# A LayerNorm's mean as two matmuls, placed later in a gemm stream, and one low weight part made by VectorE instead of by a DMA

## The chip, the core and the metric

The kernel runs on one core of a Trainium2 chip. The metric is the device time of one execution in microseconds (us); lower is better. The engines carry the names of the profile: PE is TensorE (PEld its weight loads), DVE is VectorE, ACT is ScalarE, POOL is GpSimd, SP is SyncE, which here only issues DMAs.

## The reference, cut to what matters

One layer of a decoder trunk on 288 tokens (256 of a new sequence and 8 times 4 of running ones), all in float32.

```python
h = rmsnorm(x, norm1_g)
proj = h @ w_in + b_in                         # 2048 -> 3072
a, gate, z = proj[:, :1024], proj[:, 1024:2048], proj[:, 2048:]
u = a * sigmoid(gate)
c = silu(layernorm(depthwise_causal_conv(u_ext, conv_w, conv_b), ln_g, ln_b))   # 31 taps, 1024 channels
d = multiscale_pool(z_ext)                     # windows 2, 4, 8, 16
p = einsum(d, pool_w) * pool_scale             # 4 groups of 256
x = x + concat([c, p]) @ w_out                 # 2048 -> 2048
x = x + square(relu(rmsnorm(x, norm2_g) @ w_ff1)) @ w_ff2     # 2048 -> 8192 -> 2048
y = rmsnorm(x, norm_f)

def layernorm(x, g, b):
    mu = mean(x); var = mean((x - mu) ** 2)
    return (x - mu) * rsqrt(var + EPS) * g + b
```

The change is in the mean `mu` of this LayerNorm, over the 1024 channels of the convolution, and in how one piece of `w_in` is prepared.

## The kernel before, in words

Channels lie on the 128 partitions and the 288 tokens on the free axis, so every matmul has a 128x128 block of a weight matrix as its stationary side and 288 columns as its moving side. To come near float32, each weight and each activation is split in two parts of type float32r, a high one and a low one, and a product is three matmuls: high by high, low weight by high, high weight by low.

**Weights.** A weight block of 1024 rows and 256 columns comes in two halves (`load`, 512 KB each, issued by SP into the six buffers `wr`). `split_part` makes `whi` and `wlo` of a half; there are five buffers of each. ACT always makes `whi` with a cast (L260). The table `WAYS` says who makes `wlo`, half by half: `G` is POOL (two subtractions of 128x512, L268), `V` is DVE (one subtraction of 128x1024, L265), and `D` is ACT and a DMA: ACT writes the negative of `whi` into `wlo` (L262), and POOL issues a DMA that adds the weights from memory to it (L263). `turns` counts the halves of a stage, so `"c3": "GDGD"` stands for the four halves of the fourth conv projection, c3.

**Stages.** `SEQUENCE` sets the order of the input projections: c0 to c7 are pairs of a conv and a gate tile (`conv_products`, then `conv_pair`), p3 to p0 the pooling groups, P3 to P0 their small products. A `gemm` runs over k in pairs of two; one such step of two banks is 12 matmuls. In the conv tail (priority `later`) DVE applies the 31 taps of tile i one after another (L426, the tiles `pc` and, for the last tap, `c`). POOL adds finished pairs of conv tiles into `sum_c` (L435), up to tile 5.

**The output projection and the LayerNorm.** The output product is cut in two. First come eight gemms (g = 0 to 7) with the pooling half `mixp` (`dx` in the rows); each writes one pair of PSUM banks `ac` and is added to `xT` by DVE (L549). Into this stream the LayerNorm is woven: `BETWEEN` names, by gemm and k, where PE runs the matmul of the mean (`ln_mean`), the matmuls of the sum of squares (`ln_sums`, then a chain of small steps on DVE and ACT for the reciprocal root) and the matmuls that spread the result over the partitions (`ln_rows`). After the eight gemms the normalised tiles `mixc` (`mx` in the rows) are made by DVE and ACT (L554 to L560), and eight more gemms with `mixc` follow. Then the MLP, four chunks of 2048, and the final norm.

**What sets the order.** The program is put into each engine's queue by a list scheduler that follows its own estimate of times and the priorities; each engine then works through its queue in that order. So a small edit moves instructions far from it. The PSUM pool `acc` has two pairs of banks: a gemm can start when the xT add of the gemm two before it is done.

Of the kernel before, what the change touches and what calls it, by code (L numbers as in the profile page):

```python
# [12 lines left out]
ALU = mybir.AluOpType  # L13
# [17 lines left out]
N8 = DC // P  # L31
# [35 lines left out]

WAYS = {"c2": "GVGV", "c3": "GDGD", "c4": "GDGD", "p3": "GDDG", "c5": "GDGD", "c": "GGGV", "p": "GVVG", "w": "GG", "ff": "VV"}  # L70


VEC = (("norm1_g", 16), ("b_in", 24), ("conv_b", 8), ("ln_g", 8), ("ln_b", 8), ("pool_scale", 8), ("norm2_g", 16), ("norm_f", 16))
# [10 lines left out]
def trunk_kernel(ctx: ExitStack, tc: tile.TileContext, io):  # L84
# [3 lines left out]
    nc = tc.nc  # L88
# [14 lines left out]
    def nm(s):  # L103
        seen[s] = seen.get(s, 0) + 1
        return f"{s}{seen[s]}"

    @contextmanager
    def later(by=LATER):

        tc.cur_priority += by  # L110
        yield
        tc.cur_priority -= by
# [15 lines left out]
    def ms(name):  # L128
        return msp.tile([P, 2, 512], F32, name=nm(name), tag="ms")
# [8 lines left out]
    def samples(ap, n):  # L138
        return ap.rearrange("p (b t) -> p b t", t=n)
# [8 lines left out]
    def v(key, j):  # L148
        return vec[:, OFF[key] + j : OFF[key] + j + 1]
# [45 lines left out]
    ones = const.tile([P, P], F32, name="ones")  # L195
# [3 lines left out]
    def load_table(func, src):  # L199

        nc.scalar.activation(few[: src.shape[0], :], src, func)
# [52 lines left out]
    def split_part(raw, src, hi, lo, way):  # L254

        nc.scalar.copy(hi, raw)  # L260
        if way == "D":
            nc.scalar.activation(lo, f32(hi), AF.Copy, scale=-1.0)  # L262
            nc.gpsimd.dma_start(lo, src, accum_op=ALU.add)  # L263
        elif way == "V":
            nc.vector.tensor_tensor(lo, raw, f32(hi), op=ALU.subtract)  # L265
        else:
            for j in range(0, raw.shape[1], 2):
                nc.gpsimd.tensor_tensor(lo[:, j : j + 2, :], raw[:, j : j + 2, :], f32(hi[:, j : j + 2, :]), op=ALU.subtract)  # L268

    def spl():  # L270
        return [wspl.tile([P, 4, 256], F32R, name=nm("w" + part), tag="w" + part) for part in ("hi", "lo")]
# [4 lines left out]
    def split(halves, stage="ff"):  # L276

        parts = []
        for raw, src in halves:
            turns[stage] = turns.get(stage, -1) + 1  # L280
            parts.append(spl())
            ways = WAYS.get(stage) or WAYS[stage[0]]
            split_part(raw, src, *parts[-1], ways[turns[stage] % len(ways)])
        return lambda k, m: columns(*parts[k // 4], k % 4, m)

    def gemm(banks, rhs, m_outer=False, between={}, classes=""):


        n = len(rhs)
        gets = ready.pop()  # L290
        step = 2 if len(banks) == 2 else 1
        pairs = [(k, m) for k in range(0, n, step) for m in range(len(banks))]
        if m_outer:
            pairs.sort(key=lambda km: km[1])
        if step == 2:
            parts = ((0, 0, 0), (1, 0, 0), (0, 1, 0), (1, 1, 0), (1, 0, 1), (0, 0, 1))
        else:
            parts = ((0, 0, 0), (0, 0, 1), (0, 1, 0))
        todo = [(k + d, m, w, x) for k, m in pairs for d, w, x in parts]
        head = todo[: len(classes)]  # L300
        for j, c in enumerate(classes):
            todo[j] = next(p for p in head if (p[0] + p[3]) % 2 == int(c))
            head.remove(todo[j])
        ends = {m: [f(j for j, p in enumerate(todo) if p[1] == m) for f in (min, max)] for m in range(len(banks))}
        ahead = None
        for j, (k, m, w, x) in enumerate(todo):
            if j % (len(banks) * len(parts)) == 0:
                ahead = between[k]() if k in between else None
            with tc.issue_after(ahead.ins) if ahead is not None else nullcontext():
                last = nc.tensor.matmul(banks[m][:, :T], gets[k // 8](k % 8, m)[w], rhs[k][x], start=j == ends[m][0], stop=j == ends[m][1])  # L310
        ready.extend(itertools.islice(weights, 1))
        return last.ins
# [4 lines left out]
    def each(bk):  # L317
        return [bk[:, m, :] for m in range(2)]
# [72 lines left out]
    cs, pcs = [], []  # L391
    sum_c = tmpp.tile([P, 2, T], F32, name="sum_c", tag="ag2", bufs=2)
# [10 lines left out]
    def conv_pair(i, banks):  # L403
        up = u_all[:, i, 0:UO]
        us = samples(u_all[:, i, UO:UL], US)
        ta, gate = [b[:, :T] for b in banks]
        for b in (gate, ta):
            nc.vector.tensor_tensor(b, b, rb, op=ALU.mult)
        tg = tmpp.tile([P, 2, T], F32, name=nm("tg"), tag="ag", bufs=2)[:, 0, :]
        nc.scalar.activation(tg, gate, AF.Sigmoid, bias=v("b_in", 8 + i))  # L410
        if i == N8 - 1:
            load_table(AF.Sqrt, tg[:, 0:1])
        for out, a, b in ((up[:, CH:UO], ta[:, :SEQ], tg[:, :SEQ]), (us[:, :, CH:US], samples(ta[:, SEQ:T], NS), samples(tg[:, SEQ:T], NS))):
            nc.vector.scalar_tensor_tensor(out=out, in0=a, scalar=v("b_in", i), in1=b, op0=ALU.add, op1=ALU.mult)
        if i % 2 == 0:
            cs.append(actp.tile([P, 2, T], F32, name=nm("c"), tag="c", bufs=4))
        c = cs[i // 2][:, i % 2, :]
        with later():
            if i % 2 == 0:
                pcs.append(cvp.tile([P, 2, SEQ], F32, name=nm("pc"), tag="cv"))  # L420
            pc = pcs[i // 2][:, i % 2, :]
            cwv = vec[:, CWO + i * CW : CWO + (i + 1) * CW]
            nc.scalar.activation(pc, up[:, 0:SEQ], AF.Identity, bias=v("conv_b", i), scale=cwv[:, 0:1])  # L423
            for w in range(1, CW):
                dst = pc if w < CW - 1 else c[:, 0:SEQ]
                nc.vector.scalar_tensor_tensor(out=dst, in0=up[:, w : w + SEQ], scalar=cwv[:, w : w + 1], in1=pc, op0=ALU.mult, op1=ALU.add)  # L426
            prd = prdp.tile([P, NB, NS, CW + 1], F32, name=nm("prd"), tag="prd")
            nc.scalar.activation(prd[:, :, :, CW], ones[:, 0 : NB * NS].rearrange("p (b t) -> p b t", t=NS), AF.Identity, bias=v("conv_b", i), scale=0.0)
            for t in range(NS):
                nc.gpsimd.tensor_tensor(prd[:, :, t, 0:CW], us[:, :, t : t + CW], cwv[:, None, :].to_broadcast([P, NB, CW]), op=ALU.mult)  # L430
            cso = c[:, SEQ:T]
            nc.vector.tensor_reduce(samples(cso, NS), prd, axis=AX.X, op=ALU.add)
            if i % 2 and 1 < i < N8 - 1:
                for m in range(2):
                    nc.gpsimd.tensor_tensor(sum_c[:, m, :], (cs[0] if i == 3 else sum_c)[:, m, :], cs[i // 2][:, m, :], op=ALU.add)  # L435


    dd = {}
# [58 lines left out]
    with tc.issue_after(gemm(pair0 + pair1, hx, between={15: first_sums})):  # L497
        third = conv_products(2, between={2: first_rows})
    nc.gpsimd.memset(z_all[:, :, 0:PH], 0.0)
    conv_pair(0, pair0)  # L500
    conv_pair(1, pair1)
    conv_pair(2, third)
    for kind, i in SEQUENCE[3:]:
        if kind == "c":
# [10 lines left out]
    norm = {}  # L515

    def ln_mean():
        nc.vector.tensor_tensor(sum_c, sum_c, cs[-1], op=ALU.add)  # L518
        nc.vector.tensor_tensor(sum_c[:, 0, :], sum_c[:, 0, :], sum_c[:, 1, :], op=ALU.add)  # L519
        norm["mean"] = ms("pmean")[:, 0, :T]  # L520
        return nc.tensor.matmul(norm["mean"], ones, sum_c[:, 0, :], start=True, stop=True)  # L521

    def ln_sums():
        ssc = None
# [13 lines left out]
        norm["rows"], last = spread(norm["sums"])  # L538
        return last

    BETWEEN = {4: {4: ln_mean}, 5: {6: ln_sums}, 6: {4: ln_rows}}
    behind = nullcontext()
    for g in range(8):
        bk = bank2()
        with behind:
            last = gemm(each(bk), [mixp[k] for k in korder], between=BETWEEN.get(g, {}))
        behind = tc.issue_after(last) if g > 3 else nullcontext()
# [4 lines left out]
    for j, c in enumerate(cs):  # L552
        n = tmpp.tile([P, 2, T], F32, name=nm("n"), tag="ag", bufs=2)
        nc.vector.tensor_tensor(n, c, norm["rows"][:, None, :].to_broadcast([P, 2, T]), op=ALU.mult)  # L554
        for m in range(2):
            i = 2 * j + m
# [145 lines left out]
```

## Time and profile before

| | |
|---|---|
| median of 3 runs | 1096.75 us (1096.19 to 1097.46) |
| the profiled execution | 1097.78 us, of which the span of the profile is 1096.0 us |
| granted TensorE clock, mean | 0.994 |
| busy: PE, DVE, ACT, POOL | 1077.8, 640.9, 477.5, 179.2 us |
| read from HBM | 185.68 MB, 173 GB/s over the span |

The profile shows one execution. Times in its rows count from the start of the span. A row of the timeline gives start, duration, engine, line, operation, the written tile and the tiles read, and in brackets the idle time of the engine ahead of it with what ended it. A row of the chain of waits gives start, duration and what the end of the program waited on there. A row of windows gives, for a stretch, the busy time and number of starts of each engine, then the granted TensorE clock, the DMA share and GB/s.

### The profile page before, as it was taken

How to read it: one execution, taken by the hardware profiler on the slowest of the kernel's cores; microseconds unless marked ns; L12 is line 12 of the kernel's file. 1: busy time of each engine (PE TensorE's matmuls, PEld its weight loads, DVE VectorE, ACT ScalarE, POOL GpSimd, SP SyncE). 2: the span in 40 equal slices, each digit the busy share in tenths (PEclk: the TensorE clock that was granted, in tenths of full speed). 3: DMA queues.
4: the chain of work that ended last, by engine and by line, in shares of the span. 5: the costliest groups of instructions: out<-in, count | busy, mean ns of one | idle time of the engine just before them, and what ended most of it. 6: DMA issues, size and time to landing. Idle time of an engine off the chain costs nothing.

```text
span 1096.0 us, 19604 instructions
## 1 busy us (share of the span) xinstructions
PE 1077.8 (98%) x8204; PEld 1075.6 (98%) x8204; DVE 640.9 (58%) x814; ACT 477.5 (44%) x585; POOL 179.2 (16%) x209
## 2 busy tenths in 40 slices
PE   8999999899999999999999999999999999999996
PEld 8999999899999999999999999999999999999996
DVE  7889999778554544445554444445544445554553
ACT  8654445365444433334443333444433334444441
POOL 0878989602100000000000000000000000000000
PEclk9999999899999999999999999999999999999998
DMA  9996468455455555555555555555555555555522
GB/s 335 277 271 175 147 166 244 150 159 170 157 169 168 165 171 173 168 169 166 171 171 168 167 168 174 168 167 168 171 173 164 169 169 172 171 165 167 171 77 87
DMA packets 58264, 191.23 MB, mean 174 GB/s; under 512 B 6208, under 2 KB 11328, under 8 KB 58176
## 3 DMA queue, kind: packets, MB, share of 16 engines
q1 hardware_dynamic: 56752, 185.53, 54.0%
q0 software_dynamic: 1152, 4.19, 2.1%
q8 instruction: 64, 1.05, 0.4%
q10 hardware_dynamic: 272, 0.26, 0.1%
q14 instruction: 24, 0.20, 0.0%
HBM read 185.68 MB, written 4.28 MB: 173 GB/s over the span
## 4 chain that ended last, share of the span: by engine, by line
PE 95%; DMA 1%; DVE 1%; POOL 1%; issue 1%; ACT 0%; SPq 0%; DVEq 0%; POOLq 0%
PE ac L310 93%; DMA wlo<-in_w 1%; POOL wlo L268 1%; PE pp L310 0%; DVE xT L642 0%; DMA wr<-in_w 0%; POOL prd L430 0%; DVE sum_c L518 0%; PE pt L225 0%; ACT whi L260 0%; PE idle L228 0%; PE pt L245 0%; DVE sum_c L519 0%; PE pmean L521 0%; DVE wlo L265 0%
## 5 line engine op out<-in xcount | busy, mean ns | idle before, releaser
L260 ACT CAST whi<-wr 128x1024 fp32r<-128x1024 f32 (+1 forms) x341 | 355.1, 1041 | 566.2 <-PE ac L310 544.9
L265 DVE TENSOR_TENSOR wlo<-wr,whi 128x1024 fp32r<-128x1024 f32 (+1 forms) x295 | 363.3, 1232 | 352.5 <-ACT whi L260 352.1
L310 PE MATMUL ac<-ax,whi 128*128 128x288 f32 x2048 | 351.5, 292 | 0.0
L310 PE MATMUL ac<-fx,whi 128*128 128x288 f32 x2048 | 350.4, 292 | 0.0
L310 PEld LDWEIGHTS ac<-ax,whi 128*128 128x128 f32 x2048 | 296.0, 187 | 0.0
L310 PEld LDWEIGHTS ac<-fx,whi 128*128 128x128 f32 x2048 | 295.5, 187 | 0.0
L310 PE MATMUL ac<-ax,wlo 128*128 128x288 f32 x1024 | 217.1, 292 | 0.0
L310 PE MATMUL ac<-fx,wlo 128*128 128x288 f32 x1024 | 216.6, 292 | 0.0
L310 PEld LDWEIGHTS ac<-ax,wlo 128*128 128x128 f32 x1024 | 162.5, 187 | 0.0
L310 PEld LDWEIGHTS ac<-fx,wlo 128*128 128x128 f32 x1024 | 162.1, 187 | 0.0
L310 PE MATMUL ac<-hx,whi 128*128 128x288 f32 x768 | 136.5, 296 | 2.2 <-ACT hx L332 1.5
L310 PEld LDWEIGHTS ac<-hx,whi 128*128 128x128 f32 x768 | 114.0, 189 | 2.8 <-ACT hx L332 1.7
L268 POOL TENSOR_TENSOR wlo<-wr,whi 128x512 fp32r<-128x512 f32 x76 | 104.3, 1420 | 42.4 <-ACT whi L260 41.4
L426 DVE SCALAR_TENSOR_TENSOR pc<-u_all,vec,pc 128x256 f32<-128x256 f32 x232 | 99.7, 483 | 3.2 <-ACT pc L423 1.9
L310 PE MATMUL ac<-hx,wlo 128*128 128x288 f32 x384 | 85.5, 296 | 1.2 <-DMA wlo<-in_w 1.0
L310 PEld LDWEIGHTS ac<-hx,wlo 128*128 128x128 f32 x384 | 62.7, 189 | 1.7 <-DMA wlo<-in_w 1.3
L310 PE MATMUL ac<-dx,whi 128*128 128x288 f32 x256 | 47.6, 306 | 0.0
L310 PE MATMUL ac<-mx,whi 128*128 128x288 f32 x256 | 44.8, 296 | 0.0
L310 PEld LDWEIGHTS ac<-dx,whi 128*128 128x128 f32 x256 | 39.6, 197 | 0.3
L607 DVE SCALAR_TENSOR_TENSOR t<-ac,r 128x576 f32<-128x576 f32 x32 | 24.2, 758 | 26.4 <-PE ac L310 25.3
L310 PEld LDWEIGHTS ac<-mx,whi 128*128 128x128 f32 x256 | 37.7, 189 | 0.0
L636 DVE TENSOR_TENSOR xT<-xT,ac 128x576 f32<-128x576 f32 x24 | 18.1, 754 | 19.5 <-PE ac L310 19.5
(105 smaller groups left out, 507.7 us busy)
## 6 DMA issues: line engine op xcount, KB each, us to landing
wr<-in_w SPq DMA_DIRECT2D x335, 512.0 KB, 3.8
wlo<-in_w POOLq DMA_DIRECT2D x8, 512.0 KB, 7.6
xT<-in_xT SPq DMA_DIRECT2D x7, 288.0 KB, 8.2
wr<-in_w SPq DMA_DIRECT2D x5, 256.0 KB, 3.8
out_u_out<-u_all SPq DMA_DIRECT2D x1, 1208.0 KB, 10.5
out_yT<-xT SPq DMA_DIRECT2D x2, 576.0 KB, 2.9
u_all<-in_hist_c SPq DMA_DIRECT2D x8, 136.0 KB, 5.1
out_z_out<-z_all SPq DMA_DIRECT2D x1, 668.0 KB, 8.5
```

Of the source, the lines that this page charges most:

```text
L260: nc.scalar.copy(hi, raw)
L265: nc.vector.tensor_tensor(lo, raw, f32(hi), op=ALU.subtract)
L268: nc.gpsimd.tensor_tensor(lo[:, j : j + 2, :], raw[:, j : j + 2, :], f32(hi[:, j : j + 2, :]), op=ALU.subtract)
L310: last = nc.tensor.matmul(banks[m][:, :T], gets[k // 8](k % 8, m)[w], rhs[k][x], start=j == ends[m][0], stop=j == ends[m][1])
L426: nc.vector.scalar_tensor_tensor(out=dst, in0=up[:, w : w + SEQ], scalar=cwv[:, w : w + 1], in1=pc, op0=ALU.mult, op1=ALU.add)
L607: nc.vector.scalar_tensor_tensor(out=t, in0=bk[:, :, :T], scalar=0.0, in1=both(r2), op0=ALU.max, op1=ALU.mult)
L636: nc.vector.tensor_tensor(x2, x2, bk[:, :, :T], op=ALU.add)
```

## The change

Three things are changed. In `WAYS`, the fourth half of c3 is made by DVE (`V`) and no longer by ACT and a DMA (`D`). The sum over the channels for the mean is finished early but for the last conv tile: once tile 6 is done, DVE adds the second plane of `sum_c` and tile 6 to the first plane, and `ln_mean` runs two matmuls into the same bank, one over that sum and one over tile 7, in place of two adds and one matmul. And the three steps of the LayerNorm stand later in the gemm stream: the mean at the start of gemm 5 (it stood in the middle of gemm 4), the sums in the middle of gemm 6 (late in gemm 5), the rows in gemm 7 at k = 2 (in the middle of gemm 6).

```diff
-WAYS = {"c2": "GVGV", "c3": "GDGD", "c4": "GDGD", ...
+WAYS = {"c2": "GVGV", "c3": "GDGV", "c4": "GDGD", ...
@@ conv_pair, behind POOL's sums @@
+            if i == N8 - 2:
+                for part in (sum_c[:, 1, :], c):
+                    nc.vector.tensor_tensor(sum_c[:, 0, :], sum_c[:, 0, :], part, op=ALU.add)
@@ ln_mean @@
-        nc.vector.tensor_tensor(sum_c, sum_c, cs[-1], op=ALU.add)
-        nc.vector.tensor_tensor(sum_c[:, 0, :], sum_c[:, 0, :], sum_c[:, 1, :], op=ALU.add)
         norm["mean"] = ms("pmean")[:, 0, :T]
-        return nc.tensor.matmul(norm["mean"], ones, sum_c[:, 0, :], start=True, stop=True)
+        nc.tensor.matmul(norm["mean"], ones, sum_c[:, 0, :], start=True, stop=False)
+        return nc.tensor.matmul(norm["mean"], ones, cs[-1][:, 1, :], start=False, stop=True)
@@ the places in the gemm stream @@
-    BETWEEN = {4: {4: ln_mean}, 5: {6: ln_sums}, 6: {4: ln_rows}}
+    BETWEEN = {5: {0: ln_mean}, 6: {4: ln_sums}, 7: {2: ln_rows}}
```

Lines behind the edit count three higher in the new file up to `ln_mean` and two higher after it.

The first place is POOL's queue while c3 is computed. `wlo_607` and `wlo_621` are the second and fourth half of c3, `wlo_870` is the second half of c4 (`wlo_869` in the new numbering), `prd` are products of the conv. Before:

```order
L263 DMA wlo_607<-in_w 128x1024
L430 TENSOR_TENSOR prd_709<-u_all,vec 128x8x31 x3
L268 TENSOR_TENSOR wlo_616<-wr_611,whi_615 128x512 x2
L263 DMA wlo_621<-in_w 128x1024
L268 TENSOR_TENSOR wlo_865<-wr_860,whi_864 128x512 x2
L430 TENSOR_TENSOR prd_755<-u_all,vec 128x8x31 x4
L263 DMA wlo_870<-in_w 128x1024
```

And now, POOL at the same place:

```order
L263 DMA wlo_607<-in_w 128x1024
L430 TENSOR_TENSOR prd_708<-u_all,vec 128x8x31 x3
L268 TENSOR_TENSOR wlo_616<-wr_611,whi_615 128x512 x2
L268 TENSOR_TENSOR wlo_864<-wr_859,whi_863 128x512 x2
L430 TENSOR_TENSOR prd_754<-u_all,vec 128x8x31 x4
L263 DMA wlo_869<-in_w 128x1024
```

The DMA of `wlo_621` is gone from POOL; all else stands as it did. In DVE's queue its subtraction now stands among the taps of the first conv tiles:

```order
L432 TENSOR_REDUCE c_631<-prd_664 128x32
L426 SCALAR_TENSOR_TENSOR pc_632<-u_all,vec,pc_632 128x256
L265 TENSOR_TENSOR wlo_621<-wr_613,whi_620 128x1024
L426 SCALAR_TENSOR_TENSOR pc_632<-u_all,vec,pc_632 128x256 x2
L432 TENSOR_REDUCE c_631<-prd_708 128x32
```

Where it stands there were only taps before.

The second place is the end of the conv on DVE and the mean. `c_1733` (now `c_1732`) is the last pair of conv tiles, `pc` its running sum, the `ac` are the banks of gemms 2, 3 and 4. DVE before:

```order
L549 TENSOR_TENSOR xT<-xT,ac_2419 128x576
L426 SCALAR_TENSOR_TENSOR pc_1734<-u_all,vec,pc_1734 128x256 x9
L549 TENSOR_TENSOR xT<-xT,ac_2483 128x576
L426 SCALAR_TENSOR_TENSOR pc_1734<-u_all,vec,pc_1734 128x256 x2
L426 SCALAR_TENSOR_TENSOR c_1733<-u_all,vec,pc_1734 128x256
L518 TENSOR_TENSOR sum_c<-sum_c,c_1733 128x576
L519 TENSOR_TENSOR sum_c<-sum_c 128x288
L526 TENSOR_TENSOR c_632<-c_632,pmean_2574 128x576
```

DVE now, from the two early adds on:

```order
L438 TENSOR_TENSOR sum_c<-sum_c 128x288
L426 SCALAR_TENSOR_TENSOR pc_1733<-u_all,vec,pc_1733 128x256
L438 TENSOR_TENSOR sum_c<-sum_c,c_1732 128x288
L426 SCALAR_TENSOR_TENSOR pc_1733<-u_all,vec,pc_1733 128x256 x5
L551 TENSOR_TENSOR xT<-xT,ac_2420 128x576
L426 SCALAR_TENSOR_TENSOR pc_1733<-u_all,vec,pc_1733 128x256 x10
L551 TENSOR_TENSOR xT<-xT,ac_2484 128x576
L426 SCALAR_TENSOR_TENSOR pc_1733<-u_all,vec,pc_1733 128x256 x3
L426 SCALAR_TENSOR_TENSOR c_1732<-u_all,vec,pc_1733 128x256
L551 TENSOR_TENSOR xT<-xT,ac_2548 128x576
L528 TENSOR_TENSOR c_631<-c_631,pmean_2613 128x576
```

The two adds behind the last tap are gone; two smaller ones stand some twenty taps ahead of it, four taps and not three are left behind the xT add of gemm 3, and the add of gemm 4 stands ahead of the first use of the mean. PE before, in the middle of gemm 4:

```order
L310 MATMUL ac_2547<-dx_1556,whi_2541 128x288 x2
L521 MATMUL pmean_2574<-sum_c,ones 128x288
L310 MATMUL ac_2547<-dx_1896,whi_2536 128x288 x2
L310 MATMUL ac_2547<-dx_1896,wlo_2537 128x288 x2
L310 MATMUL ac_2547<-dx_1896,whi_2536 128x288 x4
```

PE now, between gemm 4 and gemm 5:

```order
L310 MATMUL ac_2548<-dx_2063,whi_2537 128x288 x2
L522 MATMUL pmean_2613<-sum_c,ones 128x288
L523 MATMUL pmean_2613<-c_1732,ones 128x288
L310 MATMUL ac_2612<-dx_1256,whi_2606 128x288 x2
L310 MATMUL ac_2612<-dx_1256,wlo_2607 128x288 x2
```

The mean stands 24 matmuls later and has two matmuls.

The third place is where the products with `mixc` begin. `ac_2771` is the bank of gemm 7, `ac_2865` and `ac_2936` those of the first two gemms with `mixc`, `mx_2840` and `mx_2847` its first two tiles. PE before:

```order
L310 MATMUL ac_2774<-dx_2062,whi_2763 128x288 x2
L310 MATMUL ac_2865<-mx_2840,whi_2827 128x288 x2
L310 MATMUL ac_2865<-mx_2840,wlo_2828 128x288 x2
L310 MATMUL ac_2865<-mx_2840,whi_2827 128x288 x4
L310 MATMUL ac_2865<-mx_2840,wlo_2828 128x288 x2
```

PE now:

```order
L310 MATMUL ac_2771<-dx_2063,whi_2760 128x288 x2
L310 MATMUL ac_2865<-mx_2840,whi_2827 128x288 x2
L310 MATMUL ac_2865<-mx_2840,wlo_2828 128x288 x2
L310 MATMUL ac_2936<-mx_2840,whi_2918 128x288 x2
L310 MATMUL ac_2936<-mx_2840,wlo_2919 128x288 x2
L310 MATMUL ac_2865<-mx_2840,whi_2827 128x288 x4
L310 MATMUL ac_2865<-mx_2840,wlo_2828 128x288 x2
```

The first two gemms with `mixc` are now interleaved: each tile of `mixc` is used by both before the next one is asked for, and eight matmuls need only the high part of the first tile (of the four in a row that follow, the first two take its low part). DVE there, now:

```order
L556 TENSOR_TENSOR n_2836<-c_631,pt_2720 128x576
L556 TENSOR_TENSOR n_2843<-c_721,pt_2720 128x576
L265 TENSOR_TENSOR wlo_2923<-wr_2916,whi_2922 128x1024
L551 TENSOR_TENSOR xT<-xT,ac_2771 128x576
L562 TENSOR_TENSOR mx_2840<-n_2836,mx_2840 128x2x288
L562 TENSOR_TENSOR mx_2847<-n_2843,mx_2847 128x2x288
```

The xT add of gemm 7 stands ahead of the low part of the first tile; before, the add ahead of that low part was the one of gemm 6.

More of the change, by code (lines that the diff above doesn't have):

```diff
@@ L66, in weight_blocks @@
                 yield "w_ff2", r, (c, c + P)
-WAYS = {"c2": "GVGV", "c3": "GDGD", "c4": "GDGD", "p3": "GDDG", "c5": "GDGD", "c": "GGGV", "p": "GVVG", "w": "GG", "ff": "VV"}
+WAYS = {"c2": "GVGV", "c3": "GDGV", "c4": "GDGD", "p3": "GDDG", "c5": "GDGD", "c": "GGGV", "p": "GVVG", "w": "GG", "ff": "VV"}
 VEC = (("norm1_g", 16), ("b_in", 24), ("conv_b", 8), ("ln_g", 8), ("ln_b", 8), ("pool_scale", 8), ("norm2_g", 16), ("norm_f", 16))
```

## The prediction

> **What bounds the kernel now.** The page gives the engines' shares of the span first, then I read who made PE wait.
>
> ```profile
> PE 1077.8 (98%) x8204; PEld 1075.6 (98%) x8204; DVE 640.9 (58%) x814; ACT 477.5 (44%) x585; POOL 179.2 (16%) x209
> ```
>
> ```profile
> PE pmean L521 <- DVE sum_c L519: 3.2, 1, 3.2
> PE ac L310 <- DMA wlo<-in_w: 1.0, 1, 1.0
> ```
>
> PE is the bound, busy 1077.8 of 1096.0 us, so time is only won where PE waits or runs slowly. The two waits above, one at a time each, are the two that the change touches: the mean's matmul, which waited 3.2 us for DVE's second add, and one product that waited 1.0 us for a low weight part brought by DMA. The windows around them show a third loss.
>
> ```profile
> core 0: us, PE busy (x) PEld busy (x) DVE busy (x) ACT busy (x) POOL busy (x), PEclk, DMA share, GB/s
> 34.00:60.00 26.00, 24.96 (x189) 24.73 (x188) 22.01 (x49) 16.42 (x23) 21.70 (x25) 1.00 0.91 265
> 180.00:199.40 19.40, 19.39 (x146) 19.14 (x144) 16.90 (x32) 6.32 (x6) 19.40 (x17) 1.00 0.80 219
> 199.40:202.63 3.23, 0.00 (x0) 0.00 (x0) 3.15 (x2) 1.05 (x1) 3.08 (x3) 0.90 0.65 214
> 202.63:208.75 6.12, 6.11 (x23) 5.83 (x24) 3.42 (x5) 2.03 (x3) 1.08 (x1) 0.50 0.44 141
> ```
>
> At full clock 146 products take 19.40 us, 0.133 us each. After the mean's wait the clock stands at 0.50 for 6.12 us, in which only 23 matmuls start. A mean clock of 0.90 over the 3.23 us of the wait says that the fall came with a fifth of it left, some 2.6 us into the wait (0.20 x 3.23 = 0.65). The 1.04 us of idleness between 34 and 60 left the clock at 1.00. The chain of waits shows both places in order:
>
> ```profile
> 48.55 9.73 DMA wlo<-in_w
> ...
> 167.64 1.30 POOL wlo L268
> 168.95 0.04 issue
> ...
> 197.95 0.49 DVE c L426
> ...
> 198.53 2.63 DVE sum_c L518
> ...
> 201.19 1.41 DVE sum_c L519
> ...
> 202.64 1.33 PE pmean L521 x2
> 203.97 10.21 PE ac L310 x60
> 214.18 0.05 issue
> ```
>
> The DMA was issued at 48.55 and landed 9.73 us later; the last tap of the conv ends at 198.44, and both adds of the mean come between it and the matmul.
>
> **The change part by part.** *The transferred part.* In POOL's queue the DMA that goes is the second one of c3, the one of 48.55. DVE makes that part among the first taps, near 45.5 us by its place in the queue, so it is there some 10 us before PE asks for it: 1.0 us gained. What is late next is the first transferred part of c4:
>
> ```profile
> 54.24 1.41 POOL L263 DMA_DIRECT2D wlo<-in_w  x1
> ```
>
> ```profile
> wlo<-in_w POOLq DMA_DIRECT2D x1, 512.0 KB, 9.1
> ```
>
> ```profile
> 64.81 0.43 PE L310 MATMUL ac<-hx,wlo 128*128 128x288 f32 x2
> ```
>
> It landed at 63.3 (54.24 + 9.1) and was first used at 64.81, 1.5 us later; with PE 1.0 us earlier 0.5 is left. Its transfer ran beside the removed one for 4 us (54.24 to 58.28), so I expect it earlier rather than later, and take nothing for it; the bounds are 0 and the whole 1.0.
>
> ACT loses a copy and POOL an issue there; DVE gains the subtraction:
>
> ```profile
> L265 DVE TENSOR_TENSOR wlo<-wr,whi 128x1024 fp32r<-128x1024 f32 x289 | 358.3, 1240 | 348.8 <-ACT whi L260 348.4 <-issue 0.3
> ```
>
> ```profile
> 61.55 0.47 DVE L408 TENSOR_TENSOR ac<-ac,rb 128x288 f32<-128x288 f32 x1 [2.19 <-PE ac L310]
> ...
> 114.59 2.31 DVE L265 TENSOR_TENSOR wlo<-wr,whi 128x1024 fp32r<-128x1024 f32 x1
> ```
>
> It costs DVE 1.24 us by the mean of 289, and 2.3 by the one at 114.59, among taps and with POOL at work. DVE's idle 2.19 us ahead of 61.55 was a wait for PE; less the 1.0 by which PE now comes earlier, 1.2 us of it cover the addition, and at most 1.1 us of delay go on.
>
> *The mean.* Its two adds leave the path between last tap and matmul. The two that replace them stand some twenty taps earlier; each is of the form of L519, 128x288 with POOL busy, 1.4 us, 2.8 together. What covers them is DVE's last idle time before the end of the conv:
>
> ```profile
> 196.23 0.76 DVE L549 TENSOR_TENSOR xT<-xT,ac 128x576 f32<-128x576 f32 x1 [1.04 <-PE ac L310]
> ...
> 209.42 0.76 DVE L549 TENSOR_TENSOR xT<-xT,ac 128x576 f32<-128x576 f32 x1 [2.00 <-PE ac L310]
> ```
>
> So the last tap comes at 198.44 + 2.8 - 1.04 + 1.1 = 201.3 at the latest, and a good us earlier if the subtraction takes 1.24. PE reaches the mean at 199.40 - 1.0 + 24 x 0.133 = 201.6. Both are close, but the tap is ahead: the wait of 3.2 us goes. With it goes the fall of the clock. The 23 starts of that window are two of the mean and 21 products. At full clock the products take 21 x 0.133 = 2.79 us; the mean's matmul, 1.33 us at half clock, half of that, 0.67. That is 3.46 for 6.12, a gain of 2.7 us. The second matmul of the mean adds 0.67 again; the bounds are 0.27 (two ordinary products) and 1.33 (the row as it stands).
>
> The Trainium skill, "TensorE: Matmul & The Clock Gate", Part 1, says that the clock is halved after an idle window of about 3.4 us, that the windows run freely, and that one busy window frees it. By an estimate from that page the half rate could last only 3.4 us in another execution, a loss of 1.7, and the sum below would be 4.5. This trace shows the fall after 2.6 us of idleness and 6.1 us of work at half rate; the sum keeps to the trace.
>
> *The sums and rows.* From the mean to the sums PE now has 72 products, 9.6 us, where the chain shows 10.21 us for 60, with 0.05 us of waiting at 214.18. That way of 10.2 us on DVE holds the 2.00 + 0.76 us of the xT add at 209.42, waiting for gemm 4. Now the add of gemm 4 stands ahead of the mean, and the next one behind the last step, so the way is about 7.5 us: no wait. Between sums and rows there are 36 products as before.
>
> From the rows to the first product with `mixc` there were 72 products, and now there are 36, 4.8 us. What that tail took:
>
> ```profile
> 219.75 0.64 PE pt L245 x6
> ```
>
> ```profile
> 223.32 0.66 ACT L559 CAST mx<-n 128x576 fp32r<-128x576 f32 x1
> ```
>
> ```profile
> 224.32 0.75 DVE L560 TENSOR_TENSOR mx<-n,mx 128x576 fp32r<-128x576 f32 x1
> ...
> 232.28 0.75 DVE L560 TENSOR_TENSOR mx<-n,mx 128x576 fp32r<-128x576 f32 x1
> ```
>
> The rows were done at 220.39. The first high part followed 3.6 us later (223.98), the first low part 4.7 (225.07), the last low part 12.6 (233.03). Now PE wants the first high part at 4.8, the first low part eight products later, at 5.9, and, with the two gemms interleaved, the last low part after 72 + 8 more, at 15.4. All of these hold at the old pace. But DVE's queue has the xT add of gemm 7 ahead of the first low part. It can start when gemm 7 ends, at 4.8, takes 0.76, and the low part 0.75: 6.3, or 0.4 late. The same add frees the bank of the second gemm, wanted four products in, at 5.3, and free at 5.6. Together I take 0.5 us; the bounds are 0 and 2.5 (two subtractions of 1.24 ahead of it as well).
>
> *A tie.* At 168.99 PE went on 0.04 us after POOL's low part. With PE 1.0 earlier that tie may be lost: 0 to 1.0. POOL's work there was itself released by PE, so I take 0.2.
>
> **The sum.** 1.0 + 3.2 + 2.7 - 0.7 - 0.5 - 0.2 = 5.5 us. Against its own execution (1097.78, of which 1.78 lie outside the span) that is 1092.3; the median of the runs lies 1.03 lower, so the forecast is 1096.75 - 5.5 = 1091.3.
>
> **The rivals.** *The wait moves to c4.* For it: 0.5 us of slack only. Against it: less traffic on that queue. The 1.0 is lost: 1092.3. *The mean still waits*, so that the change doesn't do what it says in full. For it: DVE's margin at the mean is 0.3 us if every addition falls out long. A wait of 1.5 us, short of the 2.6 at which the clock fell, gives 1092.8. *The clock falls again* at the start of the `mixc` products, after several short waits in a row; against it stand the 1.04 us that left it at 1.00. It costs another 2.7: 1094.0. The same page of the Trainium skill, "A second HAM failure mode", describes such oscillation from short idle times between groups of matmuls; no such fall stands in this trace. *Slower: the tail of the LayerNorm.* The halved distance from rows to `mixc` is the place. Without any wait there the gain is 6.0; a wait of W costs W, and 2.7 more once it is over 2.6, so W = 3.3 decides. If the first low part came as late as the last one did, 12.6 us after the rows, W would be 6.7 and the time 1096.75 - 6.0 + 6.7 + 2.7 = 1100.2. For it: DVE and ACT share those microseconds with the casts of the next weights. Against it: the old pace of 4.7 us. If it came 9.5 us after the rows, all the time that 72 products left it, W would be 3.6 and the result about 1097, no change.
>
> **How the numbers follow.** Forecast 0.66, wait at c4 0.15, mean late 0.10, clock again 0.04, tail of 9.5 us 0.02, tail of 12.6 us 0.03. The low end is the sum without any new wait and with the cheap matmul, 6.6, from the fastest run shown: 1096.19 - 6.6, about 1089.5. The high end takes in the first three rivals, 1094.0. About 0.2%, 2.2 us, is what a measurement of this kernel can tell from no change; the line lies at 1094.6, above all cases but the last two. Faster 0.93, within 0.2% 0.04, slower 0.03.
>
> **What would show it.** In the changed profile the wait for the transferred part and that for `sum_c` are gone from PE's waits, the mean's two matmuls stand near 201.6 without idle time, the granted clock is 1.00 from 180 to 260, and PE's new waits are short ones at the first `mixc` products, named after the xT add of gemm 7 or the first low part. It is wrong if a stretch at 0.50 stands there, or a wait over 2 us at the mean or at `mixc`.

## The result, and the profile after

| | before | changed |
|---|---|---|
| median of 4 runs, us | 1096.47 | 1106.78 (three of them 1105.73 to 1107.41) |
| lowest, us | 1095.57 | 1105.73 |
| ratio, 95% interval | | 1.0091 (1.0071 to 1.0110) |
| span of the profiled execution, us | 1096.0 | 1104.4 |
| first sum of the MLP's norm (PE, L225), us from the start | 293.82 | 302.71 |

The change made the kernel 0.9% slower; 0.5% faster was forecast. In some executions of every version that was run more than once (5 of 52 executions of the kernel before, but 14 of 18 of the three versions of the last experiments, for a reason that is not known) the products of the MLP take 0.133 us instead of 0.130, about 20 us in all; the ratios given here leave these out, and where a version had no others, it is read at the last row of the table, ahead of the MLP. That row is 8.9 us later here, so the whole loss lies before it.

PE's waits in the changed kernel (total, times, longest):

```profile
PE ac L310 <- DVE xT L551: 8.8, 2, 8.6
PE ac L310 <- DMA wlo<-in_w: 3.4, 1, 3.4
```

The two waits of before are gone, and two longer ones are there: 8.6 us for an xT add of DVE in the middle of the stream, 3.4 us for the transferred part of c4. The chain of waits leads from each to a DVE operation that the change put there (start, duration, what):

```profile
45.64 7.02 DVE wlo L265
...
53.59 1.12 DVE c L432
54.71 0.37 DVE ac L408
...
55.87 0.02 ACT tg L410
...
57.71 1.05 ACT wlo L262
58.76 1.25 ACT whi L260 x2
60.01 7.30 DMA wlo<-in_w
67.31 0.04 issue
67.35 49.49 PE ac L310 x358
...
189.76 15.11 DVE sum_c L438
...
208.13 0.67 DVE xT L551
208.79 0.14 issue
208.93 7.91 PE ac L310 x48
216.84 0.48 PE pmean L522 x2
217.32 0.48 PE pmean L523 x2
```

The subtraction forecast at 1.24 to 2.3 us lasts 7.02. Behind it DVE is late with the conv tile, and ACT waits for DVE with the gate. The DMA of c4's transferred part starts at 60.01, where it started at 54.24 before. The chain puts ACT's copies last ahead of it, but ACT's copy for this part ends at 58.76. POOL's rows show the last step, four products that had waited for DVE's `u_all`, with the DMA right behind them:

```profile
57.44 2.64 POOL L430 TENSOR_TENSOR prd<-u_all,vec 128x248 f32<-128x248 f32 x4 [5.87 <-DVE u_all L414]
60.01 0.86 POOL L263 DMA_DIRECT2D wlo<-in_w  x1
```

The first early add, forecast at 1.4 us, lasts 15 us; the xT add behind it in DVE's queue is late by that, and with it the bank that PE wants.

What DVE and POOL did meanwhile stands in the timeline, first DVE, then POOL, of the changed kernel (start, duration, engine, line, operands):

```profile
45.64 7.02 DVE L265 TENSOR_TENSOR wlo<-wr,whi 128x1024 fp32r<-128x1024 f32 x1 [0.55 <-ACT whi L260]
...
189.68 15.18 DVE L438 TENSOR_TENSOR sum_c<-sum_c 128x288 f32<-128x288 f32 x1
...
205.18 0.45 DVE L438 TENSOR_TENSOR sum_c<-sum_c,c 128x288 f32<-128x288 f32 x1
```

```profile
43.55 1.03 POOL L263 DMA_DIRECT2D wlo<-in_w  x1
44.35 2.26 POOL L430 TENSOR_TENSOR prd<-u_all,vec 128x248 f32<-128x248 f32 x3
46.30 5.26 POOL L268 TENSOR_TENSOR wlo<-wr,whi 128x512 fp32r<-128x512 f32 x4
...
189.60 14.95 POOL L268 TENSOR_TENSOR wlo<-wr,whi 128x512 fp32r<-128x512 f32 x12
```

POOL's twelve subtractions begin at 189.60 and end at 204.55; DVE's add begins 0.08 us after their start and ends 0.3 us after their end. The second add, of the same size, comes when POOL is idle and takes 0.45. At c3 POOL's run ends at 51.56 and DVE's subtraction 1.1 later, about the time that it takes alone (1.23). In both cases DVE's operation ends only when POOL pauses; below it is called shut out. The profile counts this waiting as busy time of DVE.

The clock behind the two waits, in windows (the number behind POOL's is the granted clock):

```profile
67.50:80.00 12.50, 12.50 (x83) 12.50 (x84) 11.14 (x27) 6.98 (x9) 7.17 (x9) 0.86 0.96 243
...
208.90:212.00 3.10, 3.07 (x13) 3.10 (x14) 2.89 (x7) 0.00 (x0) 0.00 (x0) 0.53 0.00 0
```

The sum: at c4 the wait of 3.4 us and 1.75 us of clock (0.86 over 12.5 us from 67.5 on) against 1.0 before, +4.1; at the mean 8.6 us and 1.5 of clock (0.53 over 3.1 us from 208.9 on) against 3.2 + 2.7, +4.1; the mean's two matmuls take 0.96 us at full clock, where the 2.7 counted 0.67 for its one, +0.3; the `mixc` start adds 0.3. That is 8.8, against 8.9 at the MLP's norm and 8.4 in the span.

### The profile page after: what moved, and what is told of

Read it like the earlier page. It is cut to its first block, busy times and chain, and to the rows that moved or that the text cites. A ratio compares the mean times of both kernels' runs of the same rounds, so it can differ in the third digit from the quotient of the medians.

```text
span 1104.4 us, 19607 instructions
## 1 busy us (share of the span) xinstructions
PE 1079.6 (98%) x8206; PEld 1077.5 (98%) x8206; DVE 657.1 (59%) x815; ACT 476.4 (43%) x584; POOL 178.2 (16%) x208
## 4 chain that ended last, share of the span: by engine, by line
PE 92%; DVE 4%; DMA 1%; ACT 1%; issue 1%; POOL 0%; SPq 0%; DVEq 0%; POOLq 0%; ACTq 0%
PE ac L310 91%; DVE sum_c L438 1%; DVE pc L426 1%; DVE wlo L265 1%; DMA wlo<-in_w 1%; ACT whi L260 1%; DMA wr<-in_w 0%; PE pp L310 0%; DVE xT L644 0%; POOL wlo L268 0%; DVE xT L551 0%; DVE c L432 0%; PE idle L228 0%; PE pt L225 0%; PE pt L245 0%
## 5 line engine op out<-in xcount | busy, mean ns | idle before, releaser
L265 DVE TENSOR_TENSOR wlo<-wr,whi 128x1024 fp32r<-128x1024 f32 (+1 forms) x296 | 370.6, 1252 | 354.6 <-ACT whi L260 354.6
```

## The experiments: each part alone

The fourth half of c3 by DVE, on the kernel before:

```diff
-"c3": "GDGD"
+"c3": "GDGV"
```

> The kernel before with one edit: the fourth half of c3 is made by DVE and not by ACT and a DMA. Port theory (a DVE operation with two operands in SBUF, once it meets a running POOL operation, stays in its place until POOL's unbroken run is over): as in the changed kernel the subtraction near 45.6 us lasts about 7 us (POOL's run there ends at 51.56), PE then waits 3.4 us for the transferred part of c4 and loses 1.6 us more at the reduced clock, against 1.04 us before: 3.4 + 1.6 - 1.0 = 4.0 us slower, about 1100.5. Rival (the subtraction itself is as cheap as forecast, 1.2 to 2.3 us, and the loss at c4 comes from the edits at the mean): 1.0 us faster, about 1095.5.

Measured: ratio 1.0022 (1.0012 to 1.0031), 2.4 us slower, where 4.0 were expected. The subtraction lasts 7.02 us again, and PE waits 3.2 us for the part of c4; the clock stayed at 1.00 behind this wait, so the waits say 3.2 - 1.0 = 2.2. The port theory holds but for the clock.

The other side, the changed kernel with the transfer at c3 restored:

```diff
-"c3": "GDGV"
+"c3": "GDGD"
```

> The changed kernel with the fourth half of c3 by ACT and a DMA again, so that only the edits at the mean stand. Port theory: DVE's first early add still meets POOL's long run and lasts some 15 us, PE still waits 8.6 us for the xT add behind it; only what the subtraction at c3 cost comes back, 2.4 us by the run with that edit alone: about 1104.4. Rival (the subtraction is the main loss, and the add's 15 us follow from DVE being late after it): 1098 or below.

Measured, in the four executions that the ratio takes in (1.0081, 1.0054 to 1.0107): three took 1103.84, 1104.37 and 1104.77, as expected. The fourth, whose trace is shown, took 1092.05: the same program, 12 us faster. Its timeline, DVE and then POOL:

```profile
185.25 1.53 DVE L438 TENSOR_TENSOR sum_c<-sum_c 128x288 f32<-128x288 f32 x1
...
187.09 1.15 DVE L438 TENSOR_TENSOR sum_c<-sum_c,c 128x288 f32<-128x288 f32 x1
```

```profile
184.39 0.82 POOL L435 TENSOR_TENSOR sum_c<-sum_c,c 128x288 f32<-128x288 f32 x1
185.16 5.49 POOL L268 TENSOR_TENSOR wlo<-wr,whi 128x512 fp32r<-128x512 f32 x4
```

Here the add got through at the end of the one POOL operation that it met, and PE waited for nothing behind it. The two adds took 1.53 and 1.15 us, 2.7 together where 2.8 were forecast. So the order of the queues does not decide it: in the same place it is 1.5 us in one execution and, by the times of the others (12 us more, granted clock 0.990 to 0.992 instead of 0.996), about 15 in another. For those the add itself was not seen.

Only the later places, on the kernel before:

```diff
-BETWEEN = {4: {4: ln_mean}, 5: {6: ln_sums}, 6: {4: ln_rows}}
+BETWEEN = {5: {0: ln_mean}, 6: {4: ln_sums}, 7: {2: ln_rows}}
```

> The kernel before with only the three steps of the LayerNorm at their later places; the mean keeps its two adds behind the last tap and its one matmul, c3 keeps its transfer. Port theory: the two adds meet single POOL operations as before (2.62 + 1.40 us) and end near 202.6; PE arrives 24 products later than before, at 199.4 + 3.2 = 202.6, so the wait of 3.25 us and the 2.7 us at half clock go, 0.5 us are lost at the mixc products: 5.4 us faster, about 1091. Rival (the late places are what costs, by a starved xT add or a late LayerNorm tail): slower than before, 1098 or more.

Measured: 1092.35 to 1093.51, ratio 0.9961 (0.9948 to 0.9974), 4.3 us faster, where 5.4 were expected. The wait at the mean is gone with the two adds still behind the last tap (2.67 and 1.43 us), and 0.3 us of waiting remain at the `mixc` start. The later places do all the good of the edits at the mean, and the early sums were not needed for it.

## The experiments: is it POOL's run?

Two pauses put into POOL's run; `look` is a tile of one column:

```diff
 for part in (sum_c[:, 1, :], c):
     nc.vector.tensor_tensor(sum_c[:, 0, :], sum_c[:, 0, :], part, op=ALU.add)
+    nc.gpsimd.tensor_copy(look, sum_c[:, 0, 0:1])
```

> The changed kernel with one addition: behind each of the two early adds of DVE, POOL copies one column of the sum, so that POOL must wait for the add there. The first such copy stands four POOL subtractions (4 x 1.25 us) behind the second sum_c addition of POOL, with which the first add starts. Port theory: POOL's wait is the pause in which DVE gets through; the first add lasts about 5.3 us and not 15.2, PE's wait of 8.6 us for the xT add goes with its 1.5 us of reduced clock, 10 us faster than the changed kernel, about 1097. Rival (the add is slow of itself, by the transfers at that time, by its data or by its place in DVE's queue): it stays at 15 us, and the time at 1107 or above.

Measured, DVE and then POOL:

```profile
191.50 5.28 DVE L439 TENSOR_TENSOR sum_c<-sum_c 128x288 f32<-128x288 f32 x1
...
200.77 1.59 DVE L439 TENSOR_TENSOR sum_c<-sum_c,c 128x288 f32<-128x288 f32 x1
```

```profile
191.42 5.05 POOL L268 TENSOR_TENSOR wlo<-wr,whi 128x512 fp32r<-128x512 f32 x4
196.84 0.19 POOL L440 COPY look<-sum_c 128x1 f32<-128x1 f32 x1 [0.38 <-DVE sum_c L439]
```

The add lasts 5.28 us, four POOL operations and its own 0.3, and PE no longer waits 8.6 us for the xT add. The start of the MLP's norm comes at 295.30, 7.4 earlier than in the changed kernel (PE still waits 4.0 at c4 there). Its time, 1118.27, has the longer MLP in it (3003 products in 400 us, 3079 in the changed kernel) and can't be compared. In this execution POOL's run is what held the add, and a pause in it lets the add through.

How general that is, measured by itself in the MLP, where POOL is idle: runs of n operations that begin with one of two operands (the edit is shown shortened).

```diff
+for j in range(n):
+    if j == 0: nc.gpsimd.tensor_tensor(a, raw[:, 0:2, :], f32(hi[:, 0:2, :]), op=ALU.subtract)
+    elif kind == "two": nc.gpsimd.tensor_tensor(a, b, c, op=ALU.subtract)
+    elif kind == "one": nc.gpsimd.tensor_copy(a, b)
+    else: nc.gpsimd.memset(a, 0.0)
```

> The kernel before, with idle work added on POOL in the MLP, where POOL had none: runs of 1 to 12 unbroken operations of 128x512 that begin with the cast of a weight part, so that they meet DVE's subtractions of 128x1024 (1.23 us each there, one every 3.1 us). Kinds: subtraction of two SBUF operands (1.25 us each), copy of one, and writing zeros. Port theory: beside runs of n subtractions a DVE subtraction that comes while the run goes on lasts until the run is over, 1.2 us plus the rest of the run (for n = 12 up to 12 us); beside zeros alone it stays at 1.23. Rival (POOL and DVE take turns, operation by operation): no DVE subtraction lasts over 1.23 + 1.3 = 2.5 us, whatever n. The results are those of the reference.

Measured: the rival holds. In 13 runs of two-operand work, n up to 12, the longest DVE subtraction is 2.31 us. The run of twelve, DVE's rows at its start and POOL's:

```profile
566.63 1.71 DVE L267 TENSOR_TENSOR wlo<-wr,whi 128x1024 fp32r<-128x1024 f32 x1 [1.89 <-ACT whi L262]
...
569.76 2.19 DVE L267 TENSOR_TENSOR wlo<-wr,whi 128x1024 fp32r<-128x1024 f32 x1 [0.33 <-ACT whi L262]
571.87 1.85 DVE L626 TENSOR_TENSOR fx<-f,fx 128x576 fp32r<-128x576 f32 x1
```

```profile
565.97 21.01 POOL L275 TENSOR_TENSOR u_all<-u_all 128x512 f32<-128x512 f32 x11
```

They take turns: each DVE operation waits for one of POOL's, and POOL pays too, 1.9 us per operation instead of 1.38. Beside zeros DVE's subtraction stays at 1.23; beside copies it does so too, but there it began just ahead of the copy each time, so that a copy ahead of DVE was not measured. So the port theory as I had put it, that any unbroken run shuts DVE out to its end, is wrong. Something more must come in where it does.

The Trainium skill, "SBUF — State Buffer", section "Who interferes with whom", says that a DVE instruction with two SBUF inputs contends with a GpSimd instruction that reads SBUF, and that the shared port pair is an exclusive lock. The turns here agree; a wait over twelve instructions is not in what it says.

## The experiments: what shuts DVE out at c3

In the changed kernel POOL's rows after its DMA issue overlap: the three products end at 44.35 + 2.26 = 46.61, and the next row starts at 46.30. This was tested by taking the issue away, and then by putting a tiny one back.

```diff
-"c3": "GDGD"
+"c3": "GVGV"
```

> The kernel before with both transferred halves of c3 made by DVE (GVGV), so that POOL issues no DMA at 43.55. What it tells apart is why some DVE operations got through at the end of the one POOL operation they met (119.59 to 121.66 in the kernel before, POOL passing at 120.58) and that at 45.64 did not at six such points. Pause theory: behind POOL's DMA issue its records overlap by 0.31 us, elsewhere by 0.05, so that the port is never free between them until POOL pauses; without the issue both subtractions last at most 2.5 us, the wait of 1.0 us at c3 goes and nothing comes for it: about 1095.9. Rival (any unbroken run of POOL shuts DVE out to its end): one of the two lasts over 4 us, and the time is 1097 or more.

Measured, DVE's later subtraction and POOL's rows there:

```profile
45.55 1.75 DVE L265 TENSOR_TENSOR wlo<-wr,whi 128x1024 fp32r<-128x1024 f32 x1
```

```profile
42.93 3.29 POOL L430 TENSOR_TENSOR prd<-u_all,vec 128x248 f32<-128x248 f32 x5
46.16 4.81 POOL L268 TENSOR_TENSOR wlo<-wr,whi 128x512 fp32r<-128x512 f32 x3
```

1.75 us in place of 7.02, the overlap is 0.06, and no wait of PE stands at c3 or c4. The time is that of before within the interval (0.9991, 0.9979 to 1.0002).

The same with one small transfer issued by POOL among the products, into a tile that nobody reads, which ACT fills first:

```diff
+if i == 0:
+    look = const.tile([P, 4, 8], F32, name="look")
+    nc.scalar.activation(look, up[:, CH : CH + 32]..., AF.Copy, scale=-1.0)
+    nc.gpsimd.dma_start(look, io["w"][5][:, 0:4, 0:8], accum_op=ALU.add)
```

> The kernel before with both transferred halves of c3 made by DVE (there the later of the two subtractions lasted 1.75 us), and one small transfer issued by POOL where the large one of c3 stood: 32 columns of 4 bytes into a tile that nobody reads, behind the fifth product of the first conv pair. It tells whether POOL's issue alone makes its records overlap and shuts DVE out. Pause theory: behind the issue POOL's records overlap by about 0.3 us, and the later subtraction lasts about 7 us, to the end of POOL's run, with a wait of PE of 2 us or more behind it. Rival (the large transfer's traffic, or ACT's copy for it, slowed the subtraction): overlap 0.05, subtraction at most 2.5 us, PE as without it.

Measured, DVE and then POOL:

```profile
45.51 8.16 DVE L265 TENSOR_TENSOR wlo<-wr,whi 128x1024 fp32r<-128x1024 f32 x1
```

```profile
44.16 1.45 POOL L432 DMA_DIRECT2D look<-in_w  x1
45.18 2.44 POOL L434 TENSOR_TENSOR prd<-u_all,vec 128x248 f32<-128x248 f32 x3
47.12 5.45 POOL L268 TENSOR_TENSOR wlo<-wr,whi 128x512 fp32r<-128x512 f32 x4
```

The subtraction comes at the same moment and lasts 8.16 us, to 1.1 behind the end of POOL's run (52.57); POOL's rows overlap by 0.50; PE then waits 5.2 us, and the kernel takes 1102.01 to 1104.56 (1.0058, 1.0043 to 1.0073). POOL's issue does it and not the half megabyte: the transfer here has 16 KB.

No issue stands near the first early add. Whether its shut-out is a matter of POOL's time since its last pause was asked by leaving only the first of the two pauses:

```diff
-    nc.gpsimd.tensor_copy(look, sum_c[:, 0, 0:1])
+    if part is not c:
+        nc.gpsimd.tensor_copy(look, sum_c[:, 0, 0:1])
```

> The changed kernel with one column copied by POOL behind the first early add only; the second add meets POOL some four operations after that pause, with ten more to come. Pause theory (POOL's run shuts DVE out only where it has gone on for long without a pause: got through were those at up to 17 operations since the last one, shut out those at 22 and 32): the first add lasts 5.3 us, the second at most 2.0, and the sums at the start of the MLP come about 7.4 us earlier than in the changed kernel (302.7), as with two pauses. Rival (any unbroken run shuts DVE out to its end): the second add lasts 8 us or more, and PE waits for the xT add behind it again.

Measured: 5.28 us for the first add and 1.59 for the second, which POOL's ongoing run did not hold up, and 293.60 at the MLP's norm (its time, 1116.6, again has the longer MLP in it). The rival is out. The pause theory is not shown either: the add that got through in the run with the transfer restored stood as far behind POOL's last pause, 22 operations, as the three that did not. What decides at this place from one execution to the next stays open.

## The experiments: versions without a shut-out

The changed kernel with the early adds on POOL and the transfer at c3:

```diff
-nc.vector.tensor_tensor(sum_c[:, 0, :], sum_c[:, 0, :], part, op=ALU.add)
+nc.gpsimd.tensor_tensor(sum_c[:, 0, :], sum_c[:, 0, :], part, op=ALU.add)
```

> The changed kernel with the two early adds issued by POOL instead of DVE, and c3 with its transfer again: late places and two matmuls, but no addition of two SBUF operands on DVE ahead of the mean. Port theory: no DVE operation of over 3 us stands before 210, PE waits neither for the xT add nor for the mean: the time of the run with the late places alone (1093.5) plus 0.5 for the second matmul, about 1094. Rival (the early sums cost by their place, whoever makes them: the second one must wait for conv tile 6): PE still waits there for a low part of POOL or for the mean, 1097 or more.

Measured: 1092.87 in one execution; in the trace, which is of another, PE waits 1.1 us for c3's transferred part and neither for the mean nor, over 0.3 us, for an xT add. POOL's adds take 0.81 and 0.83 us. Expected was 1094.

The same with GVGV at c3, the whole idea of the change:

> The changed kernel with POOL issuing the two early adds and with both transferred halves of c3 made by DVE: the whole idea of the change, without a DVE operation that meets a POOL run it was seen to be shut out by. Port theory: 1091.3 to 1093, what was forecast for the change; a second matmul for the mean costs 0.5 against the places alone, so no better than those with the same halves. Rival (the idea is worth less than forecast even without the shut-outs): 1094.5 or more.

Measured: 1091.55 in one execution, as expected; in the trace, of another, the MLP's norm stands at 287.57.

The later places and GVGV on the kernel before, with the old mean:

> The kernel before with the three later places of the LayerNorm and with both transferred halves of c3 made by DVE: the two edits that showed no long DVE operation, put together. If the gains are those of waits removed, they add: 1093.5 (places alone) less what the two halves gave alone (0 to 1.0) gives 1092.5 to 1093.5, with no wait of PE over 0.5 us between 30 and 260. Rival (DVE's 2.5 us more work delay the last tap, and the mean waits for its two adds again, over 1 us): 1095 or more.

Measured: 1091.31 and 1091.44, ratio 0.9949 (0.9931 to 0.9967): 0.5% faster than before, with two edits of one line each, a little below the expected 1092.5 to 1093.5. No version that was run was faster, but the two times are two of six executions. PE's waits there, but for one of 0.2 us:

```profile
PE ac L310 <- ACT whi L260: 1.6, 2, 1.4
PE warm L206 <- DVE ones L196: 1.0, 1, 1.0
PE ac L310 <- POOL wlo L268: 0.3, 1, 0.3
PE ac L310 <- DVE xT L549: 0.3, 1, 0.3
```

The first two stand in the first 11 us, but for 0.2 us. The gains of the two edits add (0.9961 x 0.9991 = 0.9952), as they should when each removes a wait.

## Why the prediction was wrong, point by point

- **The subtraction at c3.** The failed step is "It costs DVE 1.24 us by the mean of 289, and 2.3 by the one at 114.59". It measured 7.02, and 7.02 to 7.19 in the four profiles with that edit. I took the longest of the rows of its kind for an upper bound, though that row got through after one operation of POOL, and at c3 a DMA issue of POOL stands ahead, with the last products and four subtractions still to come. "At most 1.1 us of delay go on" failed with it; the place was right, c4's transferred part.
- **The early adds.** The failed step is "each is of the form of L519, 128x288 with POOL busy, 1.4 us, 2.8 together": 15.18 + 0.45. It came out once, by luck, in the execution of 1092.05. The sign was in the trace of before: L518 took 2.62 us for what took L549, of the same size, 0.76, and POOL was busy beside it. L518 ended at 201.15, behind a pause of 0.15 us that POOL made at 200.54, two operations after the start of the add. A row that is 3.4 times as long as its like suggests that its length is another engine's, and the bound is then the rest of POOL's run, 12 x 1.25 = 15 us, not the row. With that bound the rival on the slower side would have been this one.
- **The waits of before.** Both went, as forecast; the new waits were worse. The clock of 1.00 from 180 to 260 did not come: it stands at 0.50 from 205.0 to 211.8.
- **The clock's 2.7** is that of one execution. The same wait of the mean was followed by 3.41 us at half clock in the kernel with only the fourth half of c3 by DVE, which loses 1.7, and by none in the one with the small transfer (3.16 us of waiting).
- **The second matmul** took 0.48 us at full clock (0.67 was taken). **The `mixc` start** cost 0.3 (0.5), by the xT add that was named. **The tie** at POOL's low part cost nothing in the changed kernel (0.2).
- **The sum** of 5.5 is borne out for what it counted, but not closely: without a shut-out the idea gave 1091.55, where 1091.3 was forecast, in one execution, with GVGV at c3 and the adds on POOL. That it comes so near is in part luck, as the clock's term shows. The rival of the LayerNorm's tail did not come up.

## What to carry to other kernels

When a two-operand SBUF operation of DVE is put beside a stretch in which POOL is never idle, take the time to POOL's next pause for its upper bound, whatever similar rows took; look in the trace for such rows that are longer than their size explains, and see whose end they follow. Keep it away from POOL's DMA issues above all, or give the sum to POOL, where it took 0.8 us for each add here. A wait can be removed by moving the reader later, which adds no work to any engine: try this alone first.

## What the runs showed of the hardware that I had not expected

- Behind a DMA issue on POOL at c3, its next operations overlap in the records by 0.31 us (512 KB) and 0.50 us (16 KB), and a DVE subtraction of 1.23 us waited for the whole run, 7.0 to 8.2 us, in each of the five profiles that have it. How the overlap brings the waiting about was not tested.
- The same program can be shut out at one place in one execution and, by its times, not in the next, 12 us apart.
- Beside one-operand copies of POOL, DVE kept 1.23 us, and POOL paid: a copy followed the one before after 0.69 us, and after 1.75 where DVE came between. In all four meetings DVE had begun first, by 0.02 us at most, so this shows only that a copy waits for DVE. Beside zeros neither paid (1.23, and 0.58 for each).
- The fall of the clock has no fixed price. After 3.2 us without work at c4 it stayed at 1.00 in one kernel; after 3.4 us there it was 0.86 over 12.5 us in another; and after 8.6 us of waiting it cost 1.5 us, less than the 2.7 after 3.2 us in the kernel before. The clock records of the traces show what goes with it. The changes of the clock in one trace lie whole multiples of 3.413 us apart, so each trace can be divided into stretches of that length, counted from any change. From 20 us on, every stretch at full clock in which PE was idle for 1.9 us or more ends with a fall to half clock, and none does in which it was idle for 1.64 or less. Between 20 and 1000 us there are nine falls in the thirteen traces, and half clock then lasts for one stretch, 3.41 us (five falls), or two, 6.83 us (four). The wait of 3.16 us at c4, behind which nothing fell, was split by an edge into 1.57 and 1.59. The wait of 8.6 us covers 3.9 of its 6.83 us at half clock, in which there was no work to slow. The Trainium skill, "TensorE: Matmul & The Clock Gate", Part 1, says that its windows run freely; these rows agree.
